# Neighbourhood attention with 192 keys in its edge blocks, a shared transpose for the remainders, later pieces of the weight sums, and two adds of the feed-forward products moved to VectorE

## The chip, the cores and the metric

The kernel runs on one core of one Trainium2 chip. The metric is the device time of one execution in microseconds (us). Before the change it was 1300.42 us, the median of three runs (1299.76 to 1302.81).

## The reference, cut to what matters

The reference is a two-layer encoder over 512 tokens of width 1024, all in f32. The tokens form a grid of 8 rows by 64 columns. Each layer does three residual steps. The first is a mixer, which adds the output of eight heads of neighbourhood attention and of eight heads of grouped-query attention. The second is a cross-attention over 256 memory tokens, and the third a feed-forward block with a gated unit, a convolution of width three over the positions and two products. The step that the change rewrites is the neighbourhood attention: each query sees all 8 rows and a window of 16 columns, clamped at the borders.

```
row_start = clip(r - kh // 2, 0, rows - kh)            # kh = 8 = rows: all rows
col_start = clip(c - NA_KW // 2, 0, GRID_W - NA_KW)    # NA_KW = 16
col_valid = (c[None] >= col_start[:, None]) & (c[None] < col_start[:, None] + NA_KW)
scores = q.k * dh ** -0.5 + bias[h, row_off, col_off]
scores = where(col_valid, scores, -1e30)
o = softmax(scores, over rows and columns) . v
```

## The kernel before, in words

**Tiling.** The tokens are reordered column by column, so 128 tokens are 16 columns of all 8 rows. The 512 queries make four blocks of 128. The keys that a block's queries can see lie in at most 32 columns, so each block takes a window of 256 keys that starts at key 0, 64, 192 or 256 (`WIN`, line 48). Blocks 0 and 3 lie at the border: the last 64 keys of block 0's window and the first 64 of block 3's are beyond the reach of every query, and their bias is -1e30.

**Number format.** All large products are made of f32 operands that are split into a high and a low part (hi is a rounded copy, made by ScalarE, lo is the difference, made by VectorE or GpSimd); three products hi·hi, hi·lo, lo·hi are summed in PSUM (`mm3`, line 939). Weights come from HBM into a `raw` tile and are split by `emit_split` (lines 801 and 802).

**Units of the neighbourhood attention.** A unit is a pair of heads and a pair of query blocks, so 8 units per layer and 16 in all; `bp` = 0 has blocks 0 and 1, `bp` = 1 has blocks 2 and 3, so each unit has one edge block and one inner block. A unit has four steps. `na_scores` (line 1405) makes eight score matmuls, then for each head and block one VectorE operation that adds the bias and takes the maximum over 256 columns (line 1423), and one exponential on ScalarE (line 1429). `na_normalise` (line 1433) scales the four blocks by the reciprocal sums, one on ScalarE and three on GpSimd (line 1106). `na_transpose` (line 1444) makes four 128x128 transposes per head on TensorE into one PSUM bank (line 1451), which ScalarE and VectorE split into hi and lo (lines 1099 and 1100). `na_values` (line 1459) makes eight value matmuls and folds the results (lines 1475 to 1477).

**The value tiles.** For each group of four heads (`g` = 0 and 1) the values, split into hi and lo, lie in four tiles `vs[0..3]` of two blocks of 128 keys each. `vs[0]` and `vs[1]` hold the keys from 0, 128, 256 and 384. `straddle` (line 1390) copies halves of them between partitions, with five DMAs, to the blocks that start at keys 64, 192 and 320 (`vs[2]` and the first half of `vs[3]`). The second half of `vs[3]` is unused.

**What sets the order.** `weave` (line 196) calls the unit's steps in a software pipeline; between them a filler runs other matmuls (projections, memory values, output rows), paced by `NA_FILL`. Work that must come later is put in `late`, a list with due times in TensorE nanoseconds (n times `LATE` = 3600). All DMAs of SP keep the written order. For the compute engines a planner (class `Order`, line 359) simulates the whole program with its own cost figures, with random draws from a fixed seed, and fixes the order of TensorE, VectorE, ScalarE and GpSimd from the best of its rounds; any change of the program makes it plan all of it anew.

**Weight sums.** The feed-forward products from tile 4 on use sums and differences of weight quarters. `make_form` (line 717) makes one piece of them in HBM: SP issues a copy (line 730), and GpSimd issues an accumulating DMA on it (line 731). Pieces are made at given steps of the stages: in both layers' neighbourhood attention at steps 0 to 4 of ten (line 1733), then in the later stages. In the first layer, steps 0 to 6 also run `mem_stat` (line 1157), which loads the memory tokens with SP in four pieces and squares each on ScalarE (line 1164).

**Feed-forward products.** `up_forms` (line 1977) combines partial products per tile `j` (4 to 21, 18 per layer). At two places a half bank is copied from PSUM to SBUF by ScalarE (lines 2033 and 2045), GpSimd adds another half to it (lines 2034 and 2046), and VectorE adds the result into a bank (lines 2035 and 2047).

Of the kernel before, what the change touches and what calls it, by code (L numbers as in the profile page):

```python
# [11 lines left out]
F32 = mybir.dt.float32  # L12
F32R = mybir.dt.float32r
AF = mybir.ActivationFunctionType
# [33 lines left out]
WIN = [0, 64, 192, 256]  # L48
WTYPE = [0, 1, 1, 2]

# [6 lines left out]

NA_FILL = [[2800] * 6 + [1500] * 4, [2800] * 6 + [1400] * 4]
GQA_SLOT = [3750] * 16 + [4200, 3300]
MEM_FILL = [1, 1, 2, 2, 1, 3, 1, 3, 1, 3, 1]  # L60
# [635 lines left out]
def encoder_kernel(ctx: ExitStack, tc: tile.TileContext, t: dict, out: bass.AP):  # L696
# [521 lines left out]
    for l in range(DEPTH):  # L1218
# [6 lines left out]
        def load_bias(p):  # L1225
            bias[p] = [rtile((4, 256), F32) for _ in range(2)]
            for j in range(2):
                SP.dma_start(bias[p][j][:, 0:3, :], t["bias"][l, 2 * p + j])

# [160 lines left out]
        def straddle(g, vs):  # L1390
            straddled[g] = True
            for dst, src in (
                (vs[2][0:64, 0:2], vs[0][64:128, 0:2]),
                (vs[2][64:128, 0], vs[0][0:64, 1]),
                (vs[2][64:128, 1], vs[1][0:64, 0]),
                (vs[3][0:64, 0], vs[1][64:128, 0]),
                (vs[3][64:128, 0], vs[1][0:64, 1]),
            ):
                SP.dma_start(f(dst), f(src))


# [3 lines left out]
        def na_scores(u):  # L1405
# [11 lines left out]
            nmx, sums = small(4), small(4)  # L1417
            es = [tmp((2, 256)) for _ in range(2)]
            for j in range(2):
                for i in range(2):  # L1420
                    b = 2 * bp + i
                    col = slice(2 * j + i, 2 * j + i + 1)
                    DVE.tensor_tensor_reduce(  # L1423
                        out=sc[j][:, i, :], in0=sc[j][:, i, :], in1=bias[p][j][:, WTYPE[b], :],
                        op0=ALU.add, op1=ALU.min, scale=-1.0, scalar=BIG, accum_out=nmx[:, col])
            for j in range(2):
                for i in range(2):
                    col = slice(2 * j + i, 2 * j + i + 1)
                    ACT.activation(es[j][:, i, :], sc[j][:, i, :], AF.Exp, bias=nmx[:, col], scale=-1.0,  # L1429
                                   accum_out=sums[:, col])  # L1430
            na[u] = es, sums

        def na_normalise(u):
            es, sums = na[u]
            DVE.reciprocal(sums, sums)
            for j in range(2):
                for i in range(2):
                    if i or j:
                        normalise(es[j][:, i, :], sums, 2 * j + i, POOL)
                    else:  # L1440
                        ACT.activation(es[j][:, i, :], es[j][:, i, :], AF.Copy, scale=sums[:, 2 * j + i : 2 * j + i + 1])
            na[u] = es

        def na_transpose(u):
            es = na[u]
            pts = []
            for j in range(2):
                tr = ps_t()
                for i in range(2):
                    for c in range(2):  # L1450
                        PE.transpose(tr[:, (2 * i + c) * P : (2 * i + c + 1) * P], es[j][:, i, c * P : (c + 1) * P], ident)  # L1451
                pt = rtile((2, S))
                split_psum(pt[:, 0, :], pt[:, 1, :], tr)
                pts.append(pt)
            na[u] = pts

        o32s = {}

        def na_values(u):
# [7 lines left out]
            for j in range(2):  # L1467
                po = ps_mm().rearrange("p (i n q) -> p i n q", i=2, n=2)
                for i in range(2):
                    b = 2 * bp + i  # L1470
                    for c in range(2):
                        PE.matmul(po[:, i], vblk[p // 2][WIN[b] + P * c][:, 2 * (p % 2) + j, :],
                                  pts[j][:, :, (2 * i + c) * P : (2 * i + c + 1) * P], start=c == 0, stop=c == 1)
# [252 lines left out]
        def na_quanta(s):  # L1726
# [250 lines left out]
        def up_forms(j):  # L1977
# [66 lines left out]
            product(c, "diffs", 0, "b22", False)  # L2044
            ACT.copy(vc, cl)  # L2045
            POOL.tensor_add(vc, vc, u2)  # L2046
            DVE.tensor_add(bl, ch, vc)
# [178 lines left out]
def _bias_index():  # L2226
# [11 lines left out]
    return np.broadcast_to(ro[:, None, :], ci.shape), ci  # L2238

# [42 lines left out]
```

## Time and profile before

| what | value |
|---|---|
| median of three runs | 1300.42 us (1299.76 to 1302.81) |
| the profiled execution's own time | 1298.67 us |
| its span, first to last instruction | 1296.9 us |
| TensorE (PE) busy | 1285.7 us, 6731 matmuls |
| VectorE (DVE) busy | 919.5 us |
| ScalarE (ACT) busy | 786.9 us |
| GpSimd (POOL) busy | 861.0 us |
| mean granted TensorE clock | 0.999 |
| DMA moved | 241.22 MB, mean 186 GB/s |

The profile names engines PE (matmul), PEld (weight load), DVE (VectorE), ACT (ScalarE), POOL (GpSimd) and SP (SyncE, which issues DMAs); a name with a q at its end is the engine's sequencer. An instruction is told as line, engine, operation, out<-in. L103 is the helper line behind which all counted matmuls stand; L80 is that for operations that keep the written order, the DMAs of SP among them. Ends of matmuls are modelled and overlap, so the distance from one start to the next tells what a matmul costs, and the duration does not.

### The profile page before, as it was taken

The numbers are of one execution on the slowest core, as the hardware profiler recorded it, in microseconds if no ns is written. First come the engines' busy times: TensorE is split into PE (matmuls) and PEld (weight loads), VectorE is DVE, ScalarE is ACT, GpSimd is POOL, SyncE is SP. The second block draws the span as 40 slices with busy tenths as digits, with TensorE's granted clock in tenths as the row PEclk, the third lists the DMA queues.
The fourth block names the chain that finished last, engine by engine and source line by source line (L and its number), as shares of the span: only waits on it lengthen the run. The fifth ranks groups of instructions, "written<-read, shape, count | busy, mean of one in ns | idle before, by whom it ended". The sixth has DMA issues, their size and how long they took to land.

```text
span 1296.9 us, 19575 instructions
## 1 busy us (share of the span) xinstructions
PE 1285.7 (99%) x6731; PEld 1093.9 (84%) x6731; DVE 919.5 (71%) x1727; ACT 786.9 (61%) x1487; POOL 861.0 (66%) x656
## 2 busy tenths in 40 slices
PE   9999999999999999999999999999999999999997
PEld 8888888888888888888888888888888888888887
DVE  6568977677986765866635697776789767667565
ACT  6667867566655654554636687765656556456444
POOL 3658966736777776766746579757367766667663
PEclk9999999999999999999999999999999999999999
DMA  9998496497985465554459965946988855555441
GB/s 290 283 281 202 131 246 144 151 257 195 244 210 146 140 179 146 166 159 131 146 164 270 287 152 159 240 109 225 219 223 207 206 155 158 162 158 154 144 134 65
DMA packets 293698, 241.22 MB, mean 186 GB/s; under 512 B 7776, under 2 KB 249952, under 8 KB 293600
## 3 DMA queue, kind: packets, MB, share of 16 engines
q1 hardware_dynamic: 276288, 201.83, 51.7%
q0 software_dynamic: 16896, 37.75, 16.2%
q8 instruction: 53, 0.87, 0.3%
q10 hardware_dynamic: 416, 0.39, 0.1%
q14 instruction: 45, 0.37, 0.1%
HBM read 229.99 MB, written 77.59 MB: 237 GB/s over the span
## 4 chain that ended last, share of the span: by engine, by line
PE 95%; DVE 2%; ACT 1%; DMA 1%; issue 0%; POOL 0%; POOLq 0%; SPq 0%; DVEq 0%; ACTq 0%
PE mm L103 69%; PE sc L103 18%; PE tr L103 5%; PE tr L1606 2%; PE tr L1451 1%; PE tr L1802 1%; DMA r<-r 0%; DVE sc L1423 0%; PE tr L1521 0%; DVE r L1317 0%; DMA xT<-in_xT 0%; DVE r L1300 0%; ACT t L1429 0%; ACT hi L801 0%; DVE r L1100 0%
## 5 line engine op out<-in xcount | busy, mean ns | idle before, releaser
L802 POOL TENSOR_TENSOR lo<-raw,hi 128x512 fp32r<-128x512 f32 (+3 forms) x329 | 576.4, 1769 | 257.1 <-ACT hi L801 209.9
L801 ACT CAST hi<-raw 128x1024 fp32r<-128x1024 f32 (+2 forms) x369 | 295.5, 815 | 273.3 <-issue 64.8
L103 PE MATMUL mm<-r,hi 128*128 128x512 f32 (+1 forms) x1376 | 419.3, 389 | 0.0
L103 PEld LDWEIGHTS mm<-r,hi 128*128 128x128 f32 x1376 | 249.4, 188 | 43.9
L103 PE MATMUL mm<-r,lo 128*128 128x512 f32 (+1 forms) x864 | 261.9, 345 | 0.0
L103 PE MATMUL mm<-xg,hi 128*128 128x512 f32 x768 | 228.0, 392 | 0.0
L103 PEld LDWEIGHTS mm<-r,lo 128*128 128x128 f32 x864 | 152.1, 188 | 26.6 <-DVE lo L802 1.7
L103 PEld LDWEIGHTS mm<-xg,hi 128*128 128x128 f32 x768 | 140.6, 188 | 26.7
L103 PE MATMUL mm<-xg,lo 128*128 128x256 f32 (+1 forms) x528 | 139.5, 331 | 0.0
L103 PE MATMUL mm<-hi,xg 128*128 128x512 f32 (+1 forms) x384 | 111.1, 360 | 1.5 <-DVE r L1300 1.5
L103 PEld LDWEIGHTS mm<-xg,lo 128*128 128x128 f32 x528 | 89.2, 188 | 15.4
L1106 POOL TENSOR_SCALAR t<-t,s 128x512 f32<-128x512 f32 (+1 forms) x112 | 67.5, 620 | 41.4 <-DVE s L1590 21.1
L2046 POOL TENSOR_TENSOR t<-t 128x256 f32<-128x256 f32 x36 | 43.1, 1197 | 71.9 <-ACT t L2045 71.9
L103 PE MATMUL sc<-xg,hi 128*128 128x512 f32 x304 | 88.8, 393 | 0.2 <-ACT xg L80 0.2
L103 PEld LDWEIGHTS mm<-hi,xg 128*128 128x128 f32 x384 | 68.1, 189 | 10.6 <-DVE r L1300 1.7
L802 DVE TENSOR_TENSOR lo<-raw,hi 128x1024 fp32r<-128x1024 f32 (+1 forms) x40 | 54.5, 1362 | 31.2 <-ACT hi L801 31.2
L103 PE MATMUL sc<-r,r 128*128 128x256 f32 (+1 forms) x352 | 74.1, 331 | 0.0
L1099 ACT CAST r<-tr 128x512 fp32r<-128x512 f32 x79 | 45.5, 587 | 37.9 <-DVE tr L1916 27.0
L103 PE MATMUL mm<-lo,xg 128*128 128x512 f32 (+1 forms) x192 | 68.5, 357 | 0.0
L2053 DVE TENSOR_TENSOR sc<-mm,t 128x256 f32<-128x256 f32 x36 | 15.6, 432 | 74.1 <-ACT t L2052 74.1
L103 PEld LDWEIGHTS sc<-xg,hi 128*128 128x128 f32 x304 | 55.0, 189 | 10.7 <-ACT xg L80 0.5
L1100 DVE TENSOR_TENSOR r<-tr,r 128x512 fp32r<-128x512 f32 x79 | 53.4, 685 | 13.0 <-ACT r L1099 9.4
(232 smaller groups left out, 2389.9 us busy)
## 6 DMA issues: line engine op xcount, KB each, us to landing
raw<-in_w_up SPq DMA_DIRECT2D x52, 512.0 KB, 4.6
raw<-dr_sums SPq DMA_DIRECT2D x36, 512.0 KB, 4.0
raw<-dr_diffs SPq DMA_DIRECT2D x36, 512.0 KB, 4.1
raw<-in_w_in SPq DMA_DIRECT2D x25, 512.0 KB, 6.2
raw<-in_w_down SPq DMA_DIRECT2D x32, 384.0 KB, 3.8
dr_sums<-in_w_up SPq DMA_DIRECT2D x8, 1280.0 KB, 8.6
dr_diffs<-in_w_up SPq DMA_DIRECT2D x8, 1280.0 KB, 8.6
raw<-in_w_up SPq DMA_DIRECT2D x36, 256.0 KB, 3.2
```

The source lines that it names most:

```text
L103: return self.engine.matmul(out, lhsT, rhs, **k)
L801: act.copy(hi[:, k], raw[:, k])
L802: (POOL if eng[0] == "P" else DVE).tensor_sub(lo[:, k], raw[:, k], f(hi)[:, k])
L1099: ACT.copy(hi, ps)
L1100: DVE.tensor_sub(lo, ps, f(hi))
L1106: eng.tensor_scalar(e, e, sums[:, col : col + 1], 1.0, op0=ALU.mult, op1=ALU.mult)
L1451: PE.transpose(tr[:, (2 * i + c) * P : (2 * i + c + 1) * P], es[j][:, i, c * P : (c + 1) * P], ident)
L1606: PE.transpose(tr[:, k * P : (k + 1) * P], es[j][:, k * P : (k + 1) * P], ident)
L1802: PE.transpose(tr[:, (2 * c + i) * P : (2 * c + i + 1) * P], e[:, i, c * P : (c + 1) * P], ident)
L2046: POOL.tensor_add(vc, vc, u2)
L2053: DVE.tensor_add(ch, ah, l4)
```

## The change

Block 0 uses keys 0 to 191 and block 3 keys 320 to 511, which is 192 keys. The score matmuls stay 256 wide, but the bias addition, the exponential and the normalisation of an edge block take 192 columns, and the bias array in HBM has 640 columns for its three kinds of block where it had 768. The two heads' edge blocks lie side by side in one tile (`edge`, 384 columns). 192 keys are one transpose of 128 and a remainder of 64; the remainders of the two heads are neighbours in `edge` and go through one transpose, so a unit has 7 transposes where it had 8, and the second bank to be split is 384 wide. The value matmul of the remainder has 64 keys of the one head and 64 of the other on its partitions. So its stationary operand (`rest`) has the head's own values on 64 partitions and zeros on the other 64. `heads_apart` makes such a block with six DMAs: two copies of values and four of zeros. The block for the lower edge goes into the unused half of `vs[3]`, directly after `straddle`. The block for the upper edge goes over the keys from 128 in `vs[0]`, which no value matmul reads any more, three `late` steps after that, or when unit 1 of the group of four has been transposed. The number of value matmuls is still eight.

The pieces of the weight sums in the first layer's neighbourhood attention move from steps 0 to 4 to steps 3 to 7; the second layer keeps steps 0 to 4. In `up_forms`, for tiles from 7 on (15 of 18 per layer), the copy by ScalarE and the addition by GpSimd become one addition by VectorE, at both places.

```diff
+KEYS = [slice(0, 192), slice(0, 256), slice(0, 256), slice(64, 256)]
+EDGE = {0: (0, 64), 3: (320, 384)}
+BIAS = [slice(0, 192), slice(192, 448), slice(192, 448), slice(448, 640)]
...
+REST = 3
+NA_SUMS = [(3, 4, 5, 6, 7), (0, 1, 2, 3, 4)]
...
+    zeros = cpool.tile([P, 64], F32R, name="zeros")
+    DVE.tensor_sub(zeros, ident[:, 0:64], ident[:, 0:64])
...
+            kept_vs[g] = vs
+            rest[g][0] = vs[3][:, 1]
+            heads_apart(vs[3][:, 1], (vs[0][0:64, 1], vs[0][0:64, 0]))
+            late(REST, lambda: last_rest(g, vs))
...
+        def heads_apart(dst, srcs):
+            dst = dst.rearrange("p (a j) d -> p a j d", j=2)
+            for j, src in enumerate(srcs):
+                src = src.rearrange("p (a j) d -> p a j d", j=2)
+                r, o = slice(64 * j, 64 * j + 64), slice(64 - 64 * j, 128 - 64 * j)
+                SP.dma_start(f(dst[r, :, j]), f(src[:, :, j]))
+                for i in range(2):
+                    SP.dma_start(f(dst[o, :, j, 64 * i : 64 * i + 64]), f(zeros[o].unsqueeze(1).to_broadcast([64, 2, 64])))
+
+        def last_rest(g, vs):
+            if rest[g][1] is None:
+                rest[g][1] = vs[0][:, 1]
+                heads_apart(vs[0][:, 1], (vs[1][64:128, 1], vs[1][64:128, 0]))
...
-                        out=sc[j][:, i, :], in0=sc[j][:, i, :], in1=bias[p][j][:, WTYPE[b], :],
+                        out=sc[j][:, i, ks], in0=sc[j][:, i, ks], in1=bias[p][j][:, BIAS[b]],
...
-                for i in range(2):
-                    for c in range(2):
-                        PE.transpose(tr[:, (2 * i + c) * P : (2 * i + c + 1) * P], es[j][:, i, c * P : (c + 1) * P], ident)
+                ins = [es[j][1 - bp][:, 0:P], es[j][1 - bp][:, P : 2 * P], edge[:, 256 * j : 256 * j + P], edge[:, P : 2 * P]]
+                n = len(ins) - j
+                for c, e in enumerate(ins[:n]):
+                    PE.transpose(tr[:, c * P : c * P + P], e, ident)
...
+                    if b in (0, 3):
+                        assert rest[p // 2][bp] is not None
+                        vs = [(vblk[p // 2][EDGE[b][j]], pts[j], 2), (rest[p // 2][bp], pts[0], 3)]
+                    else:
+                        vs = [(vblk[p // 2][WIN[b] + P * c], pts[j], c) for c in range(2)]
...
-            if s in (0,1,2,3,4,):
+            if s in NA_SUMS[l]:
                 make_form()
...
-            ACT.copy(gb, bl)
-            POOL.tensor_add(gb, gb, p1)
+            if j < 7:
+                ACT.copy(gb, bl)
+                POOL.tensor_add(gb, gb, p1)
+            else:
+                DVE.tensor_add(gb, bl, p1)
...
-            ACT.copy(vc, cl)
-            POOL.tensor_add(vc, vc, u2)
+            if j < 7:
+                ACT.copy(vc, cl)
+                POOL.tensor_add(vc, vc, u2)
+            else:
+                DVE.tensor_add(vc, cl, u2)
```

More of the change, by code (lines that the diff above doesn't have):

```diff
@@ L1225, in load_bias @@
         def load_bias(p):
-            bias[p] = [rtile((4, 256), F32) for _ in range(2)]
+            bias[p] = [rtile((1024,), F32) for _ in range(2)]
             for j in range(2):
-                SP.dma_start(bias[p][j][:, 0:3, :], t["bias"][l, 2 * p + j])
+                SP.dma_start(bias[p][j][:, 0:640], t["bias"][l, 2 * p + j])
         def project_first():
@@ L1417, in na_scores @@
             nmx, sums = small(4), small(4)
-            es = [tmp((2, 256)) for _ in range(2)]
+            inner, edge = tmp((2, 256)), tmp()
+            es = [[edge[:, 192 * j : 192 * j + 192] if i == bp else inner[:, j] for i in range(2)] for j in range(2)]
+            for j in range(2):
+                for i in range(2):
+                    b = 2 * bp + i
+                    col, ks = slice(2 * j + i, 2 * j + i + 1), KEYS[b]
+                    DVE.tensor_tensor_reduce(
+                        out=sc[j][:, i, ks], in0=sc[j][:, i, ks], in1=bias[p][j][:, BIAS[b]],
+                        op0=ALU.add, op1=ALU.min, scale=-1.0, scalar=BIG, accum_out=nmx[:, col])
             for j in range(2):
@@ L1422, in na_scores @@
                     col = slice(2 * j + i, 2 * j + i + 1)
-                    DVE.tensor_tensor_reduce(
-                        out=sc[j][:, i, :], in0=sc[j][:, i, :], in1=bias[p][j][:, WTYPE[b], :],
-                        op0=ALU.add, op1=ALU.min, scale=-1.0, scalar=BIG, accum_out=nmx[:, col])
-            for j in range(2):
-                for i in range(2):
-                    col = slice(2 * j + i, 2 * j + i + 1)
-                    ACT.activation(es[j][:, i, :], sc[j][:, i, :], AF.Exp, bias=nmx[:, col], scale=-1.0,
+                    ACT.activation(es[j][i], sc[j][:, i, KEYS[b]], AF.Exp, bias=nmx[:, col], scale=-1.0,
                                    accum_out=sums[:, col])
-            na[u] = es, sums
+            na[u] = es, edge, sums
         def na_normalise(u):
-            es, sums = na[u]
+            es, edge, sums = na[u]
             DVE.reciprocal(sums, sums)
@@ L1438, in na_normalise @@
                     if i or j:
-                        normalise(es[j][:, i, :], sums, 2 * j + i, POOL)
+                        normalise(es[j][i], sums, 2 * j + i, POOL)
                     else:
-                        ACT.activation(es[j][:, i, :], es[j][:, i, :], AF.Copy, scale=sums[:, 2 * j + i : 2 * j + i + 1])
-            na[u] = es
+                        ACT.activation(es[j][i], es[j][i], AF.Copy, scale=sums[:, 2 * j + i : 2 * j + i + 1])
+            na[u] = es, edge
         def na_transpose(u):
-            es = na[u]
-            pts = []
+            es, edge = na[u]
+            pts, bp = [], u % 2
             for j in range(2):
                 tr = ps_t()
-                for i in range(2):
-                    for c in range(2):
-                        PE.transpose(tr[:, (2 * i + c) * P : (2 * i + c + 1) * P], es[j][:, i, c * P : (c + 1) * P], ident)
+                ins = [es[j][1 - bp][:, 0:P], es[j][1 - bp][:, P : 2 * P], edge[:, 256 * j : 256 * j + P], edge[:, P : 2 * P]]
+                n = len(ins) - j
+                for c, e in enumerate(ins[:n]):
+                    PE.transpose(tr[:, c * P : c * P + P], e, ident)
                 pt = rtile((2, S))
-                split_psum(pt[:, 0, :], pt[:, 1, :], tr)
+                split_psum(pt[:, 0, : n * P], pt[:, 1, : n * P], tr[:, : n * P])
                 pts.append(pt)
             na[u] = pts
+            if u % 4 == 1:
+                last_rest(u // 4, kept_vs[u // 4])
         o32s = {}
@@ L1470, in na_values @@
                     b = 2 * bp + i
-                    for c in range(2):
-                        PE.matmul(po[:, i], vblk[p // 2][WIN[b] + P * c][:, 2 * (p % 2) + j, :],
-                                  pts[j][:, :, (2 * i + c) * P : (2 * i + c + 1) * P], start=c == 0, stop=c == 1)
+                    if b in (0, 3):
[3 more added lines that the diff above has]
+                        vs = [(vblk[p // 2][WIN[b] + P * c], pts[j], c) for c in range(2)]
+                    for c, (v, pt, n) in enumerate(vs):
+                        PE.matmul(po[:, i], v[:, 2 * (p % 2) + j, :], pt[:, :, n * P : n * P + P], start=c == 0, stop=c == 1)
                 r = slice(64 * j, 64 * j + 64)
@@ L2237, in _bias_index @@
         ci[:, y] = np.where((k0 + kc >= s0) & (k0 + kc < s0 + 16), dc + 15, 31)
-    return np.broadcast_to(ro[:, None, :], ci.shape), ci
+    ro = np.broadcast_to(ro[:, None, :], ci.shape)
+    return tuple(np.concatenate([v[:, 0, :192], v[:, 1], v[:, 2, 64:]], axis=1) for v in (ro, ci))
 def kernel(**inputs):
```

2 lines of the change are left out of this document (1 added, 1 removed).

## The prediction

> **What bounds the kernel.** I read the page first: how full the engines are, and the chain that ended last.
>
> ```profile
> span 1296.9 us, 19575 instructions
> ...
> PE 1285.7 (99%) x6731; PEld 1093.9 (84%) x6731; DVE 919.5 (71%) x1727; ACT 786.9 (61%) x1487; POOL 861.0 (66%) x656
> ...
> PE 95%; DVE 2%; ACT 1%; DMA 1%; issue 0%; POOL 0%; POOLq 0%; SPq 0%; DVEq 0%; ACTq 0%
> ```
>
> TensorE is busy for 99% of the span and holds 95% of the chain. So only two things shorten the time: fewer TensorE instructions, or less of TensorE's idle time, which is 1296.9 - 1285.7 = 11.2 us. Work taken from VectorE, ScalarE or GpSimd counts only where TensorE waits for it. Second I asked who TensorE waited for (us in total, times, longest):
>
> ```profile
> PE mm L103 <- DVE r L1300: 1.5, 1, 1.5
> PE tr L103 <- POOL ident masks.py:199: 1.4, 1, 1.4
> PE tr L1451 <- DVE r L1317: 0.8, 1, 0.8
> PE tr L1606 <- DVE r L1317: 0.4, 1, 0.4
> PE mm L103 <- POOL lo L802: 0.3, 1, 0.3
> ```
>
> The 1.4 us is the start, before the change has any say. The other four make 3.0 us. Third, busy time by stretches (us; PE, PEld, DVE, ACT, POOL, the clock, DMA share, GB/s), to see where the idle time lies:
>
> ```profile
> 50.00:75.00 25.00, 23.55 (x123) 19.93 (x122) 15.01 (x37) 15.85 (x39) 19.81 (x22) 1.00 1.07 317
> 100.00:125.00 25.00, 24.00 (x142) 20.37 (x141) 22.01 (x56) 18.46 (x52) 19.02 (x22) 1.00 0.91 215
> 125.00:150.00 25.00, 25.00 (x131) 20.68 (x131) 23.91 (x48) 21.87 (x45) 23.86 (x23) 1.00 0.49 145
> 450.00:625.00 175.00, 175.00 (x907) 149.04 (x906) 115.90 (x186) 90.79 (x141) 121.17 (x73) 1.00 0.54 152
> 750.00:775.00 25.00, 24.71 (x147) 20.79 (x146) 23.98 (x57) 20.56 (x50) 17.83 (x21) 1.00 0.61 121
> 775.00:800.00 25.00, 24.63 (x125) 20.01 (x124) 22.54 (x46) 22.34 (x47) 23.59 (x23) 1.00 0.46 144
> 1275.00:1296.90 21.90, 15.32 (x106) 13.90 (x104) 9.90 (x24) 10.70 (x27) 5.64 (x6) 0.95 0.27 96
> ```
>
> The last row holds 21.9 - 15.32 = 6.6 us of the idle time, at the end of the program, which the change leaves as it is. The first layer's neighbourhood attention loses 1.45 + 1.0 us, the same stage of the second layer 0.29 + 0.37 us. In the feed-forward stretch from 450 to 625 TensorE is idle for nothing. So at most some 3 us of waits can be had, all in the two attention stages.
>
> **Part 1: the transposes.** Instructions in order of time, and the row of the line:
>
> ```profile
> 94.05 1.07 PE L1451 MATMUL tr<-ident,t 128*128 128x128 f32 x8
> 94.87 0.49 PE L103 MATMUL mm<-hi,xg 128*128 128x512 f32 x1
> ...
> L1451 PE MATMUL tr<-ident,t x128: 270/272/328, 58.9 to 771.3; 128*128 128x128 f32 x128
> ```
>
> The 128 are 16 units of 8. One lasts 272 ns, but eight of them and the step to the next product take 94.87 - 94.05 = 0.82 us, so one costs 0.10 us of TensorE's time; from inside the run of eight it is (1.07 - 0.27) / 7 = 0.114 us. I take 0.108. Sixteen fewer save 16 x 0.108 = **1.7 us** (1.6 to 1.8). Score and value matmuls keep their number and width, so nothing else leaves TensorE. The Trainium skill (TensorE: Matmul & The Clock Gate, Part 4: PE-mode transpose) tells about 275 ns for a 128x128 transpose inside a kernel. Taken as the price, that would be 4.4 us; the row has the same duration, but the next start comes after 0.10 us, so it is no price here.
>
> **Part 2: narrower edge blocks.** Rows of VectorE and ScalarE (count, busy us, mean ns of one):
>
> ```profile
> L1423 DVE CUSTOM_DVE_ANT_0 sc<-sc,r 128x256 f32<-128x256 f32 x64 | 25.5, 452 | 8.9 <-PE sc L103 8.6
> L1100 DVE TENSOR_TENSOR r<-tr,r 128x512 fp32r<-128x512 f32 x79 | 53.4, 685 | 13.0 <-ACT r L1099 9.4 <-PE mm L103 3.3
> L1100 DVE TENSOR_TENSOR r<-mm,r 128x256 fp32r<-128x256 f32 x8 | 3.3, 416 | 0.9 <-ACT r L1099 0.9
> ```
>
> From 256 to 512 columns VectorE takes 685 - 416 = 269 ns more, 1.05 ns a column. Half of the 64 bias operations lose 64 columns (67 ns each) and one of two splits per unit loses 128 (134 ns): 0.27 us per unit, 4.3 us in all, with savings of the same kind on ScalarE and GpSimd. VectorE is at 22.0 and 23.9 of 25 us from 100 to 150 us, and there TensorE waits 0.8 us for its L1317 and 0.4 us again. Some three units fall there in each layer; 3 x 0.27 = 0.8 us of room. Bounds 0 to -1.2 us; I take **-0.6**, half.
>
> **Part 3: the pieces moved in the first layer.** The 1.5 us wait ended at 72.42 us. What the stage did before:
>
> ```profile
> 51.13 0.53 SPq L80 DMA_DIRECT2D dr_sums<-in_w_up  x1
> ...
> 52.89 0.46 SPq L80 DMA_DIRECT2D t<-in_memT  x1
> 53.51 0.52 SPq L80 DMA_DIRECT2D dr_diffs<-in_w_up  x1
> ...
> 61.43 0.64 ACT L1164 ACTIVATE t<-t 128x512 f32<-128x512 f32 x1 [1.37 <-DMA t<-in_memT]
> 63.18 0.69 DVE L1100 TENSOR_TENSOR r<-tr,r 128x512 fp32r<-128x512 f32 x1 [3.19 <-ACT r L1099]
> 70.95 1.41 DVE L1300 TENSOR_TENSOR r<-mm,r 64x512 fp32r<-64x512 f32 x2 [1.45 <-ACT r L1296]
> 72.42 0.50 PE L103 MATMUL mm<-hi,xg 128*128 128x512 f32 x1 [1.45 <-DVE r L1300]
> ```
>
> ScalarE stood 1.37 us in its order before L1164, for a memory load issued at 52.89 that landed at 61.4, 8.5 us later, with the DMA engines full (1.07, 317 GB/s). The rows before and behind it are copies for two pieces. VectorE then waited for ScalarE, ScalarE's next evictions were late, and TensorE lost 1.45 us. At steps 3 to 7 the first pieces come behind this load. If it lands 1.4 us earlier, the wait goes whole. Against it, the new DMAs of part 4 stand ahead of this load on SP. Bounds 0 to -1.5; I take **-1.2**.
>
> What is moved is five SP issues (0.52 us each above) and five on GpSimd:
>
> ```profile
> L731 POOL DMA_DIRECT2D dr_sums<-in_w_up x8 | 8.9, 1108 | 0.0
> ```
>
> About three of them now fall from 100 to 150 us: 3 x 1.1 = 3.3 us of GpSimd's time, where it has 50 - 19.0 - 23.9 = 7.1 us idle. I cost them at nothing; without that cover, the lo parts of weights (L802) are late by up to 3.3 us.
>
> **Part 4: the remainder blocks.** `heads_apart` is called four times per layer, with six DMAs: 24 more on SP per layer. Their nearest rows:
>
> ```profile
> 101.26 3.43 SPq L80 DMA_DIRECT2D r<-r  x5
> 104.78 0.55 SPq L80 DMA_DIRECT2D raw<-in_w_out  x1
> ...
> r<-r SPq DMA_DIRECT2D x8, 128.0 KB, 7.4
> ...
> 112.47 1.12 PE L103 MATMUL mm<-r,r 128*128 128x256 f32 x8
> ```
>
> Five such copies took 3.43 us to issue, so six take 4.1 us. Behind them on SP stand the raw weights, the copies of k and the memory loads. Raw weights are loaded as soon as one of five buffers is free and wait for GpSimd's lo, so 4 us there is hidden. The critical one is the first layer's second group: the copies of `straddle` were issued until 104.69 and take 7.4 us to land, about 112, and the first value products of that group start at 112.47. The lower-edge block is issued behind them, so it lands some 4.1 us later, at 116. Only the edge half of that unit needs it, and the planner can put filler products there. Bounds 0 to +4.1 us per layer, +8.2 for two; I take **+0.3**, near the lower end, because the planner knows these DMAs and TensorE's stretch here is more than half filler. The Trainium skill (DMA: Bandwidth & Descriptors, Rules for kernel authors) says to join small transfers, since under 64 KB one pays mostly overhead; by that these 24 are a bad trade. The trace agrees that size hardly matters here: 128 KB took 7.4 us.
>
> **Part 5: the feed-forward adds.** Fifteen of 18 tiles per layer, two places each, lose a copy and an add and gain one add, like L2043:
>
> ```profile
> L2043 DVE TENSOR_TENSOR t<-mm,t 128x256 f32<-128x256 f32 x36 | 15.1, 419 | 0.4
> L2045 ACT COPY t<-sc 128x256 f32<-128x256 f32 x36 | 13.2, 368 | 0.5
> L2046 POOL TENSOR_TENSOR t<-t 128x256 f32<-128x256 f32 x36 | 43.1, 1197 | 71.9 <-ACT t L2045 71.9
> ```
>
> VectorE gains 60 x 0.419 = 25 us, some 10 us of it in the 175 us from 450 to 625, where it has 59 us free. TensorE waits for nothing there, so the price is nothing in either direction; if VectorE were full, up to 10 us per layer would be at stake. The zero tile (one subtraction of 64 columns) costs the start 0.2 us at most; I take nothing.
>
> **The sum.** -1.7 - 0.6 - 1.2 + 0.3 = -3.2 us. The profiled execution took 1298.67 us (1.8 outside its span) and would take 1295.5. It is 1.75 us under the median of the three runs, so the forecast against the median is 1300.42 - 3.2 = **1297.2 us**, 0.25% less. About 0.3% is what a measurement of this kernel tells from no change, 3.9 us: faster means below 1296.5, slower above 1304.3.
>
> **Rivals.** *All waits go.* The planner orders anew with lighter engines and the 3.0 us vanish beside the 1.7: 1295.7; with the shorter holes that the wait list leaves out, 1294.5. For it: the second layer loses only 0.66 us with the same code, so 2.4 of the 3.0 are luck of order and of DMA load. Against it: VectorE stays above 21 of 25 us from 100 to 150.
>
> *The waits move.* The 24 DMAs fill the gap that the pieces leave, the memory load is as late as before, VectorE's stretch keeps its waits, a new order adds 1 to 2 us (the difference of the two layers shows this size): only the 1.7 is left, or nothing: 1298.7 to 1300.4.
>
> *The remainder is late.* TensorE stands at the edge product of the second group's first unit until the block lands, 4.1 us in each layer, and the moved pieces, now in flight at the same time, lengthen the 7.4 us landing by 2 us more: 8.2 + 2 - 1.7 = +8.5, 1308.9. For it: the landing at 112 and the product at 112.47 stand 0.5 us apart. It decides once the block lands later than the filler reaches, that is if fewer than 4 us of other products are ready at that place. Against it: the projections for the grouped attention run in these very microseconds.
>
> **How the numbers follow.** The forecast has 0.5, with its own range 1295.3 to 1299; about a third of that, 0.17, lies under 1296.5. All waits go 0.23, the waits move 0.16, the remainder is late 0.11. Faster is 0.23 + 0.17 = 0.40, same 0.33 + 0.16 = 0.49, slower 0.11. The range reaches from 1293.5 to 1302.0: below, all waits with the shorter holes; above, moved waits and a part of the late remainder.
>
> **What would show it.** L1451 x112 and 1.7 us less of it; edge forms of 192 columns at the bias line and the exponential; no wait of ScalarE for the memory load before 72 us, and 50 to 75 at 25 of 25; the values of the second group no later than their neighbours; the feed-forward adds of GpSimd x6 per place, and TensorE without a gap there. I am wrong if a wait for a DMA appears before a value product, if GpSimd's lo becomes TensorE's wait after 100 us, or if the saving is more than the transposes and the listed waits together.

## The result, and the profile after

The changed kernel takes 1316.45 us (median of four runs, 1314.93 to 1319.16), the kernel before 1300.1 us on the same chip. The ratio is 1.0131, with a 95% interval from 1.0116 to 1.0146: it became **slower by 1.3%**, 16 us, where the forecast was 1297.2 and the upper end of the range 1302.0. The profiled execution took 1314.93 us. Its span is 16.3 us longer than that of before. The page of the changed kernel:

```profile
span 1313.2 us, 19545 instructions
...
PE 1286.8 (98%) x6715; PEld 1096.0 (83%) x6715; DVE 942.1 (72%) x1788; ACT 767.6 (58%) x1427; POOL 803.5 (61%) x596
...
PEclk9998999999999999999999989999999999999999
...
PE 88%; DMA 6%; DVE 1%; POOL 1%; issue 1%; ACT 1%; SPq 1%; POOLq 0%; ACTq 0%; DVEq 0%
```

TensorE's idle time is now 1313.2 - 1286.8 = 26.4 us, where it was 11.2: 15.2 us more. Its busy time rose by 1.1 us although it has 16 instructions less. The granted clock shows two dips (fourth and 24th slice), and DMA holds 6% of the chain where it held 1%. Who TensorE waited for (us in total, times, longest):

```profile
PE mm L107 <- DMA r<-zeros: 16.5, 3, 10.5
PE tr L107 <- POOL ident masks.py:199: 1.4, 1, 1.4
PE mm L107 <- DVE t L1512: 0.9, 2, 0.5
PE tr L1641 <- DVE r L1323: 0.5, 1, 0.5
PE tr L1480 <- DVE r L1323: 0.3, 1, 0.3
```

Without the 1.4 us of the start this makes 18.2 us, where before had 3.4 (the 3.0 of the prediction's rows and two waits of 0.2 that it does not show): 14.8 more, nearly the whole growth of the idle time. 16.5 of the 18.2 are waits of a new kind, for the zeros that `heads_apart` writes by DMA into a remainder block. Five of the prediction's stretches (PE, PEld, DVE, ACT, POOL, the clock, DMA share, GB/s):

```profile
50.00:75.00 25.00, 25.00 (x134) 21.43 (x133) 15.78 (x42) 15.71 (x39) 18.60 (x21) 1.00 0.92 281
100.00:125.00 25.00, 17.64 (x105) 15.03 (x103) 20.57 (x49) 14.03 (x39) 16.70 (x20) 0.92 0.98 263
125.00:150.00 25.00, 21.11 (x107) 17.71 (x108) 16.83 (x32) 16.00 (x35) 15.44 (x16) 0.87 0.47 132
450.00:625.00 175.00, 175.00 (x918) 149.91 (x917) 125.74 (x211) 85.82 (x118) 99.08 (x52) 1.00 0.54 153
750.00:775.00 25.00, 19.55 (x114) 16.63 (x113) 21.09 (x55) 13.87 (x37) 18.97 (x23) 0.96 0.99 226
```

The early wait of the first layer is gone (25.00 of 25 from 50 to 75), the feed-forward stretch is as full as before, and the loss sits where the second group's edge products stand, at the same place in both layers. The instructions of TensorE there, in order of time, and those behind the wait:

```profile
117.07 0.60 PE L1556 MATMUL tr<-ident,t 128*128 128x128 f32 x4
117.43 0.60 PE L107 MATMUL mm<-r,r 128*128 128x256 f32 x3
128.54 0.55 PE L107 MATMUL mm<-r,r 128*128 128x256 f32 x1 [10.52 <-DMA r<-zeros]
...
130.60 1.02 PE L107 MATMUL mm<-hi,xg 128*128 128x512 f32 x2
131.46 0.41 PE L107 MATMUL mm<-lo,xg 128*128 128x512 f32 x1
...
132.60 0.39 PE L107 MATMUL mm<-lo,xg 128*128 128x512 f32 x1
132.83 0.63 PE L107 MATMUL mm<-hi,xg 128*128 128x512 f32 x2
```

Three value products, then 10.5 us of nothing until the third of the block's six DMAs has landed, at 128.41 (the first head's half needs these three). After it, two products of 512 columns take 131.46 - 130.60 = 0.86 us, 0.43 each; from 132.60 they take 0.23 again. That is half the clock for some 3 us: the granted clock from 128.54 to 131.47 us is 0.50. In the second layer TensorE waits 1.7 us (until 770.47) and 4.3 us (until 775.52), and from 775.52 to 780.00 its clock is 0.50 again. Half of these 2.9 and 4.5 us, 3.7 us, is what the slow clock costs by this estimate. From the busy time one gets 2.8: with -1.7 for the transposes it makes the +1.1 seen. So it is some 3 to 4 us. The Trainium skill (TensorE: Matmul & The Clock Gate, Why this matters for your kernels) says that an idle gap of over about 3 us brings the half clock back; both long waits here are followed by it, so the trace agrees.

The DMAs issued from 111.55 to 115.56 us, the last remainder block of the second group among them (out<-in, queue, count, KB each, median us from issue to landing):

```profile
dr_sums<-dr_sums POOLq DMA_DIRECT2D x1, 1024.0 KB, 12.5
dr_diffs<-in_w_up SPq DMA_DIRECT2D x1, 1024.0 KB, 12.4
r<-r SPq DMA_DIRECT2D x2, 64.0 KB, 14.6
r<-zeros SPq DMA_DIRECT2D x4, 32.0 KB, 15.0
```

32 KB took 15 us to land. Two large transfers were under way beside it, an accumulating DMA of GpSimd (issued at 110.45) and a plain copy of SP (at 111.02), both for pieces of the weight sums. In the second layer two accumulating DMAs were issued at 759.60 and 760.36, SP had no piece's copy in front, and the six copies issued from 760.59 on landed one after the other at 767.26, 768.87, 770.33, 772.04, 773.68 and 775.43.

Sums in this stretch are not new. The kernel before issued two of them at nearly the same time, and TensorE waited there for no DMA:

```profile
112.71 1.14 POOL L731 DMA_DIRECT2D dr_diffs<-dr_sums  x1
113.46 1.44 POOL L731 DMA_DIRECT2D dr_sums<-in_w_up  x1
```

New are the block that has to land beside them and, in the first layer, SP's copy of a piece just ahead of it.

### The profile page after: what moved, and what is told of

It is laid out like the page before. It is cut to its first block, busy times and chain, and to the rows that moved or that the text cites. A ratio compares the mean times of both kernels' runs of the same rounds, so it can differ in the third digit from the quotient of the medians.

```text
span 1313.2 us, 19545 instructions
## 1 busy us (share of the span) xinstructions
PE 1286.8 (98%) x6715; PEld 1096.0 (83%) x6715; DVE 942.1 (72%) x1788; ACT 767.6 (58%) x1427; POOL 803.5 (61%) x596
## 4 chain that ended last, share of the span: by engine, by line
PE 88%; DMA 6%; DVE 1%; POOL 1%; issue 1%; ACT 1%; SPq 1%; POOLq 0%; ACTq 0%; DVEq 0%
PE mm L107 63%; PE sc L107 17%; PE tr L107 5%; DMA r<-zeros 3%; PE tr L1641 2%; DMA dr_sums<-in_w_up 2%; SPq L84 1%; POOL lo L806 1%; DMA r<-r 1%; DMA raw<-in_w_in 1%; PE tr L1837 1%; PE tr L1480 0%; ACT hi L805 0%; DVE r L1323 0%; DVE r L1106 0%
## 5 line engine op out<-in xcount | busy, mean ns | idle before, releaser
L1112 POOL TENSOR_SCALAR t<-t,s 128x512 f32<-128x512 f32 (+2 forms) x112 | 66.2, 607 | 62.1 <-DVE s L1463 30.9
L1105 ACT CAST r<-tr 128x512 fp32r<-128x512 f32 (+1 forms) x79 | 43.7, 564 | 39.4 <-DVE tr L1951 28.6
L107 PEld LDWEIGHTS sc<-xg,hi 128*128 128x128 f32 x304 | 55.1, 189 | 10.5 <-ACT xg L84 0.5
L1106 DVE TENSOR_TENSOR r<-tr,r 128x512 fp32r<-128x512 f32 (+1 forms) x79 | 51.3, 659 | 16.5 <-ACT r L1105 16.0
L107 PE MATMUL sc<-r,hi 128*128 128x512 f32 x208 | 61.9, 397 | 0.0
L1619 ACT ACTIVATE t<-sc,s,qr 128x512 f32<-128x512 f32 x64 | 49.4, 779 | 21.0 <-DVE s L1112 20.6
L2039 DVE TENSOR_REDUCE t<-mm 128x256 f32<-128x512 f32 x72 | 49.4, 686 | 15.1 <-PE mm L107 14.9
```

The source lines that it names most:

```text
L107: return self.engine.matmul(out, lhsT, rhs, **k)
L1105: ACT.copy(hi, ps)
L1106: DVE.tensor_sub(lo, ps, f(hi))
L1112: eng.tensor_scalar(e, e, sums[:, col : col + 1], 1.0, op0=ALU.mult, op1=ALU.mult)
L1619: ACT.activation(e, sc[j], AF.Exp, bias=nmx[:, c], scale=qrs[b][:, col : col + 1], accum_out=sums[:, c])
L2039: DVE.tensor_reduce(dst, bank.rearrange("p (n c) -> p c n", n=2), axis=AX.X, op=ALU.add)
```

## The experiments

The question was why this block lands late. The theories were, in the order in which they came up: the **count** (six DMAs per block instead of two, through SP's eight semaphores in rotation), the **queue** (the 1 MB copy for a piece stands ahead of the block on SP's queue), and the **sums** (GpSimd's accumulating DMA, in flight at the same time). Each ratio is to the kernel before in the same session, which took 1298.9 us beside half_rows, no_edge, pieces_back and zeros_by_pool; 1300.64 beside half_rows_paired, idle_dmas, rest_from_act and pieces_away; 1299.16 beside sums_held, extra_copy and zeros_by_pool_held; and 1298.91 beside one_sum_ahead.

**half_rows: no zeros at all.** The remainder is multiplied by a 64-row matmul on its own half of the partitions, and two copies of `straddle` per group replace the twelve DMAs.

```diff
...
+                        vs = [(vblk[p // 2][EDGE[b][j]], pts[j], 2, slice(0, P)),
+                              (own, pts[0], 3, slice(64 * j, 64 * j + 64))]
...
-                        PE.matmul(po[:, i], v[:, 2 * (p % 2) + j, :], pt[:, :, n * P : n * P + P], start=c == 0, stop=c == 1)
+                        PE.matmul(po[:, i], v[h, 2 * (p % 2) + j, :], pt[h, :, n * P : n * P + P], start=c == 0, stop=c == 1)
```

> The whole change, but the shared remainder is multiplied by values that stand on 64 partitions alone, so no zeros and no block of its own are needed: two more copies in the straddle step take the place of twelve DMAs per group, and all are issued before the pieces that come later. Queue theory (TensorE stands for remainder DMAs that lie in SP's queue behind a 1 to 1.3 MB copy of a piece): no wait for the remainder, 1294 to 1299 us. Number theory (twelve small DMAs per group are too many for SP): the same, 1294 to 1299. Order theory (a new order of the engines costs the time, the DMA is only the last to come): stays above 1305.

1304.28 us, ratio 1.0041 [1.0030, 1.0052]. No wait of TensorE for a remainder is left. What stayed is a new price. TensorE's eight value products of a unit, and the group of the 64-row ones:

```profile
66.21 1.89 PE L106 MATMUL mm<-r,r 128*128 128x256 f32 x8
67.93 0.39 PE L106 MATMUL mm<-hi,xg 128*128 128x512 f32 x1
...
L106 PE MATMUL mm<-r,r 64*128 64x256 f32 x32 | 12.2, 381 | 0.0
```

The eight take 67.93 - 66.21 = 1.72 us, where they took 0.95 before; two of them are 64-row products, so one adds (1.72 - 0.95) / 2 = 0.385 us, and 32 of them 12.3 us. TensorE's busy time shows it: 1294.0 us. So the loss of the changed kernel does hang on these DMAs, and most of what this version saves on them it pays to TensorE.

**half_rows_paired.** The two 64-row products of a unit stand next to each other, behind the six others.

```diff
+                        if b in (0, 3) and c == 1:
+                            last.append(one)
+                        else:
+                            PE.matmul(*one[:3], start=c == 0, stop=c == 1)
+            for one in last:
+                PE.matmul(*one[:3], start=False, stop=True)
```

> half_rows with the unit's two 64-row products moved next to each other, behind the six full ones, so that a unit has one run of half-array products where it had two. In half_rows each 64-row product was followed by a start 0.19 us late and preceded by another (eight value products took 1.72 us where they took 0.95). If the price is for the change between full and half array: it halves, 16 times 0.38 us, 6 us less, 1297 to 1300. If it is a price of each 64-row product: no change, 1303 to 1305.

1300.32 us, ratio 0.9998 [0.9988, 1.0009]; TensorE busy 1289.8 us. Half as many changes between full and half rows cost some 4 us less, of the 6 expected. The eight products of a unit, issued from 66.35 us, take 1.12 us until the next one starts, where they took 1.72. So most of the price belongs to the change from the one form to the other, and little to the product.

**no_edge: the moved pieces and the feed-forward adds alone.** The kernel before with parts 3 and 5.

```diff
-            if s in (0,1,2,3,4,):
+            if s in ((3, 4, 5, 6, 7), (0, 1, 2, 3, 4))[l]:
                 make_form()
...
+                DVE.tensor_add(gb, bl, p1)
...
+                DVE.tensor_add(vc, cl, u2)
```

> The kernel before with only the other two parts: the first layer's pieces at steps 3 to 7 and the adds on VectorE for tiles from 7 on. No edge blocks of 192 keys. Queue and number theory: no remainder, so no such wait; 1296 to 1300 us, the first layer's stretch from 50 to 75 us without idle time of TensorE. Order theory: slower than 1303.

1297.82 us, ratio 1.0002 [0.9987, 1.0018]. Six of ten runs lay at 1297.1 to 1297.9, four at 1302.2 to 1302.6; the profiled one was of the latter and waited 3.8 us for VectorE's r L1317. From 50 to 75 us TensorE is busy for 25.00 of 25. So the two parts don't bring the loss, but no gain is seen either: in the profiled execution, what the moved pieces gain in the first stretch comes back as other waits.

**pieces_back: the whole change, with the pieces of the first layer at steps 0 to 4.**

```diff
-NA_SUMS = [(3, 4, 5, 6, 7), (0, 1, 2, 3, 4)]
+NA_SUMS = [(0, 1, 2, 3, 4), (0, 1, 2, 3, 4)]
```

> The whole change, but the first layer's pieces at steps 0 to 4 as before. Queue theory: no SP copy of a piece is issued just ahead of the last remainder block in the first layer, so its 10.5 us wait falls to at most the 6.3 us that the second layer has with the same steps: 1309 to 1313 us. Number theory: the twelve DMAs are still there, the wait stays 9 to 11 us: 1315 to 1317.

1320.37 us, ratio 1.0166 [1.0136, 1.0195]: not better, as the queue theory had it, but worse. The DMAs issued from 121.0 to 125.2 us, with the last remainder block:

```profile
dr_sums<-in_w_up POOLq DMA_DIRECT2D x1, 1024.0 KB, 13.9
raw<-in_w_out SPq DMA_DIRECT2D x1, 512.0 KB, 12.6
r<-r SPq DMA_DIRECT2D x1, 256.0 KB, 12.7
r<-r SPq DMA_DIRECT2D x2, 64.0 KB, 13.8
r<-zeros SPq DMA_DIRECT2D x4, 32.0 KB, 13.9
```

No copy of SP for a piece is among them, and the block takes 14 us all the same. What is there is an accumulating DMA of GpSimd (issued at 122.19, another at 119.33): SP's copies had moved, but GpSimd's sums stood at this place again, as in the kernel before. Beside that, TensorE lost 3.9 + 1.4 us before 91 us, and ScalarE stood 3.33 and 3.35 us for the memory load: what part 3 said of the pieces at steps 0 to 4 is seen here.

**zeros_by_pool: GpSimd writes the zeros, two DMAs per block.**

```diff
-                for i in range(2):
-                    SP.dma_start(f(dst[o, :, j, 64 * i : 64 * i + 64]), f(zeros[o].unsqueeze(1).to_broadcast([64, 2, 64])))
+                for a in range(2):
+                    POOL.tensor_copy(dst[o, a, j, :].rearrange("p (i d) -> p i d", i=2), zeros[o].unsqueeze(1).to_broadcast([64, 2, 64]))
```

> The whole change, but the zeros are written by GpSimd (four copies of 64 partitions by 128 columns per block) and only the two copies of values per block are DMAs. Number theory: a third of the DMAs is left and the waits of 16.5 us fall to a third: 1303 to 1307 us. Queue theory: the two copies lie behind the same piece and land only the time of four zero fills earlier, 2 to 3 us per layer: 1309 to 1314.

1296.67 us, ratio 0.9979 [0.9968, 0.9990], less than either theory gave. The two copies of the last block were issued at 111.67 and 112.32 and landed after 5.7 us; the accumulating DMA came only at 115.73. SP's copy of a piece still stood ahead of them (109.33). Two things had changed at once, the count and the moment of GpSimd's sums.

**idle_dmas: the count alone.** zeros_by_pool with four DMAs of 16 bytes per partition per block, into a tile that nothing reads.

```diff
...
+                    SP.dma_start(f(spare[o, c]), f(zeros[o, 0:4]))
...
```

> zeros_by_pool (zeros written by GpSimd, 1296.67 us) with four DMAs per block put back that move nothing of use: 16 bytes on each of 64 partitions into a spare tile that nothing reads. Slot theory (SP has eight DMAs in flight; each further issue waits until the one eight places before has landed, so the four extra DMAs per block push the copies of values, and what stands behind them, later by several us): the waits for the remainder come back, to 1308 to 1317 us. Data theory (what costs is that the value products need the zeros' own landing): nothing waits for these DMAs, so the time stays 1296 to 1299.

1297.94 us, ratio 0.9984 [0.9970, 0.9998]; the interval overlaps that of zeros_by_pool. Six DMAs per block on SP again, and 1.6 us of waits in all, for the copies of values. The count by itself is not the cause. The rule that the prediction weighed, to join small transfers (the Trainium skill, DMA: Bandwidth & Descriptors, Rules for kernel authors), would have had 32 more of them in the kernel cost something; beside the measurement's own spread they cost 1.3 us or nothing.

**rest_from_act: the last block's six DMAs on ScalarE's queue.**

```diff
-        def heads_apart(dst, srcs):
+        def heads_apart(dst, srcs, by=SP):
...
-                heads_apart(vs[0][:, 1], (vs[1][64:128, 1], vs[1][64:128, 0]))
+                heads_apart(vs[0][:, 1], (vs[1][64:128, 1], vs[1][64:128, 0]), ACT_IN_ORDER)
```

> The whole change, but the six DMAs of the last block of each group are issued by ScalarE's queue; the first block's six stay on SP. Slot theory: the block stands neither behind SP's eight slots nor behind a piece on SP's queue and lands in some 3 to 8 us from its issue; the waits of TensorE for it fall under 3 us and the time to 1297 to 1303 (ScalarE pays 24 issues of about 0.6 us). If instead the DMA engines are simply full at that time, whoever issues: the landing stays over 12 us, 1310 or more.

1320.99 us, ratio 1.0164 [1.0143, 1.0184]. The waits of TensorE:

```profile
PE mm L107 <- DVE r L1106: 15.1, 2, 14.5
PE mm L107 <- DMA r<-zeros: 5.8, 2, 3.5
```

The block's copies, issued from 114.29 to 132.6 us:

```profile
r<-r ACTq DMA_DIRECT2D x2, 64.0 KB, 7.0
r<-zeros ACTq DMA_DIRECT2D x4, 32.0 KB, 6.4
```

So the other queue does help the landing, as the slot theory had it: 6 to 7 us at the median, with two of GpSimd's sums in flight (issued at 109.88 and 117.09), where SP's queue took 15. What came late were the issues: 114.29, 114.98, 115.62, then 121.21, 127.57 and 132.03. In the trace ScalarE's DMAs use the same eight semaphores as SP's, and the last three issues each came 0.02 us after a DMA of SP had landed: raw weights at 121.19, copies for two pieces at 127.55 and 132.01. ScalarE stood in its own order at these issues, so its evictions were late, VectorE's split behind them, and TensorE 14.5 us behind that. An engine with a part in the chain should not issue DMAs that may have to wait.

**pieces_away: no pieces in the neighbourhood attention.** All pieces of the two stages move to the steps of the grouped attention.

```diff
-NA_SUMS = [(3, 4, 5, 6, 7), (0, 1, 2, 3, 4)]
+NA_SUMS = [(), ()]
...
-            if s in (0,4,8,12,):
+            if s in (0, 2, 4, 6, 8, 10, 12, 14, 15):
```

> The whole change, with no piece of the weight sums made in the neighbourhood attention of either layer; the five go to the grouped attention with its four. The 24 small DMAs per layer stay. Queue theory in its strong form (the pieces' big copies are what the remainder waits for): the waits vanish, 1295 to 1300. Slot theory: the big copies no longer hold slots for 8 to 12 us, so most of the wait goes too, but issues still wait for weight loads eight places before: a wait of 1 to 5 us is left, 1298 to 1304. Number of issues alone (12 times 0.65 us of SP's time): the waits stay over 10 us, 1310 or more.

1305.08 us (1302.54 to 1311.7), ratio 1.0047 [1.0028, 1.0065]. No wait for a remainder is left. The DMAs issued from 111.6 to 116.4 us:

```profile
r<-r SPq DMA_DIRECT2D x2, 64.0 KB, 3.2
r<-zeros SPq DMA_DIRECT2D x4, 32.0 KB, 2.2
```

The same six copies on the same queue land in 2 to 3 us with neither SP's copies nor GpSimd's sums about. The time was lost elsewhere: the pieces crowd the later stage, where loads took over 20 us. What this kernel can't tell is which of the two, copy or sum, made the difference.

**sums_held: the whole change, GpSimd's accumulating DMAs taken out of the stage.** SP's copies stay where they were; the sums are kept and issued one per step of the grouped attention.

```diff
-        nc.gpsimd.dma_start(dst, more, accum_op=ALU.add, max_dma_last_dim=4 * P * nj)
+        held.append((dst, more, nj))
+        if not holding[0]:
+            accumulate(len(held))
...
+    def accumulate(n):
+        for dst, more, nj in held[:n]:
+            POOL_IN_ORDER.dma_start(dst, more, accum_op=ALU.add, max_dma_last_dim=4 * P * nj)
+        del held[:n]
...
+            accumulate(1)
             return [GQA_SLOT[s]]
```

> The whole change, with its 24 small DMAs per layer and its steps for the pieces, but GpSimd's accumulating DMAs of the pieces are held back in written order and issued one per step of the grouped attention; SP's copies of the pieces stay where they are. Accumulate theory (a remainder block issued while a GpSimd accumulate of 1 MB is in flight lands 6 to 17 us after its issue, one issued before it lands in 2 to 6): no accumulate is in flight, the waits for the remainder fall from 16.5 to under 5 us, 1297 to 1304. Queue theory (SP's own copy of a piece ahead of it is what it waits for): that copy is still 0.5 us ahead in the first layer, so 8 us or more of wait stay there, 1308 to 1314.

1296.13 us, ratio 0.9970 [0.9958, 0.9982]: 20 us less than the changed kernel, with all its 48 DMAs and the copy ahead of the block. Its DMAs issued from 111.4 to 115.4 us, and its wait for the block:

```profile
dr_diffs<-in_w_up SPq DMA_DIRECT2D x1, 1024.0 KB, 7.9
r<-r SPq DMA_DIRECT2D x2, 64.0 KB, 6.7
r<-zeros SPq DMA_DIRECT2D x4, 32.0 KB, 6.0
```

```profile
PE mm L107 <- DMA r<-zeros: 1.9, 1, 1.9
```

Against the rows of the changed kernel: the same copy of SP ahead, 6.0 us instead of 15.0, 1.9 us of wait instead of 16.5; the time lies below the range of either theory. So the queue alone does not make the block late, and the sums, or the new order of work that came with holding them, do. The queue still has a part in the first layer. The block lands right behind SP's copy of the piece, here at 118.93 to 119.73 behind 118.77, in the changed kernel at 125.15 to 129.65 behind 123.43. With the sums in flight that copy took 12.4 us instead of 7.9, and the block behind it was late with it.

**extra_copy: the queue alone.** zeros_by_pool with a plain copy of 1 MB, which nothing reads, issued by SP just ahead of the last block.

```diff
...
             if rest[g][1] is None:
+                SP.dma_start(spare_copy[l][g], t["w_up"][l][:512, 0:512])
```

> zeros_by_pool (1296.67 us) with one more copy of 1 MB from HBM to HBM on SP directly ahead of the copies of the last block, in both groups of both layers; nothing reads it. Queue theory: the block lands behind it, some 5 to 8 us later; the second group's waits come back with 3 to 7 us per layer, 1302 to 1311. Accumulate theory: a copy alone takes about 6 us and the block lands behind it too, but only where its product is that near: 1298 to 1304.

1295.21 us, ratio 0.9966 [0.9952, 0.9980], below the range of either theory. The DMAs from 108.9 to 111.8 us:

```profile
dr_diffs<-in_w_up SPq DMA_DIRECT2D x1, 1024.0 KB, 7.5
dr_spare<-in_w_up SPq DMA_DIRECT2D x1, 1024.0 KB, 10.1
r<-r SPq DMA_DIRECT2D x2, 64.0 KB, 8.5
```

Two megabytes ahead on the same queue instead of one make the block land after 8.5 us instead of 5.7, and TensorE wait 1.2 us. That is the price of the queue without a sum: the next one was issued at 114.82, 3.6 us behind the block's last copy.

**zeros_by_pool_held: both remedies.** zeros_by_pool with the held sums of sums_held (the two diffs together).

> A version meant to be the best: zeros by GpSimd (1296.67 us) and the accumulates held to the grouped attention. Both theories: no wait for the remainder, and the DMA engines emptier until 145 us: 1294 to 1297. If the held accumulates get in the way of the weights of the grouped attention instead: 1298 or more.

1297.88 us, ratio 0.9990 [0.9982, 0.9999]. They don't add up: with no late block left to cure, what remains is the order that the planner finds, here with 1.6 us of wait for VectorE's t L1522 and 1.5 for r L1333.

**one_sum_ahead: one accumulating DMA put back.** sums_held, and in each layer one sum of 1 MB into a buffer that nothing reads, issued by GpSimd just ahead of the second group's last block. (One plain copy fills the buffer first, in the first layer's first group.)

```diff
             if rest[g][1] is None:
...
+                if g == 1:
+                    POOL_IN_ORDER.dma_start(spare_sum, src, accum_op=ALU.add, max_dma_last_dim=4 * P * 4)
```

> The kernel with the held sums (1296.13 us, last remainder block of the second group landed 8 us after its issue), and in it one single accumulating DMA of GpSimd, 1 MB of f32, into a buffer that nothing reads, issued just ahead of the last remainder block of the second group in each layer: two such DMAs in all. The output is the same. Theory (an accumulating DMA in flight stretches the landing of the small copies beside it): the block lands 12 to 17 us after its issue, TensorE waits for it for 6 to 17 us over the two layers and runs slower for a few us after each wait; 1303 to 1315. Rival (it was the planner's order or the traffic as a whole that the holding of the sums changed): the block lands within 8 us as before, at most 3 us of wait; 1295 to 1299.

1308.78 us, ratio 1.0075 [1.0058, 1.0092]: 12.7 us more than sums_held for two DMAs. The DMAs from 113.05 to 119.1 us, with the block, and the wait:

```profile
dr_diffs<-in_w_up SPq DMA_DIRECT2D x1, 1024.0 KB, 11.4
r<-r SPq DMA_DIRECT2D x2, 64.0 KB, 9.3
r<-zeros SPq DMA_DIRECT2D x4, 32.0 KB, 7.8
```

```profile
PE mm L107 <- DMA r<-zeros: 8.8, 4, 5.6
```

From the first issue to the last landing the block takes 12 us in the first layer (113.1 to 125.1), and two of its issues take 1.76 and 1.24 us instead of 0.6. The landings themselves lengthen by less than the 12 to 17 us expected, and by less than in the changed kernel, which has a second sum close behind the first in each layer. TensorE's idle time is 7.0 us above that of sums_held and its busy time 5.7 us (granted clock 0.89 from 125 to 150 us): the half clock is nearly half of the price. Holding the sums back had also changed the order of work. That rival expected at most 3 us of wait and 1295 to 1299 us here, and falls.

The second layer shows the sums by themselves, because there SP has no copy of a piece ahead of the block. The zeros of the second group's last block in the second layer, with no sum (sums_held), one (one_sum_ahead) and two (the changed kernel):

```profile
r<-zeros SPq DMA_DIRECT2D x4, 32.0 KB, 2.5
```

```profile
r<-zeros SPq DMA_DIRECT2D x4, 32.0 KB, 8.2
```

```profile
r<-zeros SPq DMA_DIRECT2D x4, 32.0 KB, 9.4
```

## Why the prediction was wrong, step by step

**The step that failed** is part 4, the remainder blocks at +0.3 us with bounds 0 to +8.2. It measured +16.5 us of waits and some 3 to 4 us of half clock behind them, for which the sum had no term. The bound was made of the wrong things: the time that six issues take on SP (4.1 us; the six did take 3.9) and the landing time of 128 KB copies as the page of before shows them, 7.4 us. The second is not a property of the copy (the same page has 256 KB in 3.2 us and 512 KB in 4.6). It depends on what is in flight beside it: 2 to 3 us in pieces_away, 6 in sums_held, 15 in the changed kernel.

Part 3 counted about three of GpSimd's five DMAs as coming into 100 to 150 us, and asked only for GpSimd's time (3.3 us, with 7.1 free). But two were there before (112.71 and 113.46) and two after (110.45 and 117.66). What they do to the transfers beside them was never asked, though the trace of before had them within a microsecond of the first value product at 112.47. The rival of the late remainder did name the mechanism, TensorE standing at an edge product with the pieces in flight, and gave them 2 us where the landing grew by 9 (from 6.0 to 15.0); it got 0.11.

Part 4 also followed the wrong block. It worked out 116 for the lower-edge block of the second group's first unit, which landed at 111.6, and no wait for it is in the list. The second one, which `last_rest` writes behind it on SP, was the late one, at the unit after. The prediction gave that one no landing time and no first use of its own.

**The cover failed too.** "The planner knows these DMAs" was a reason for the lower end. The order it found has sums issued within 1.2 us of the block in both layers, and beside it again in pieces_back. And the filler of "more than half" of that stretch was used up: three products of the unit ran, then TensorE stood.

**Right by mechanism and size.** Part 1: the transposes are x112, and in versions without the late block TensorE is busy for 1282.1 us (extra_copy), 1283.1 (sums_held) and 1284.3 (zeros_by_pool) where it was 1285.7 before; 1.7 us less lies inside this spread, which settles it no closer. The row's duration of 272 ns (4.4 us for 16) does not. Part 2: the bias operation of 192 columns takes 373 ns against 442, and the split of 384 columns 546 against 688, as worked out; what that is worth to TensorE no run shows alone. Part 3: TensorE's wait before 72 us is gone in the changed kernel and back, at 3.9 us, in pieces_back; ScalarE's own wait for the memory load only fell, from 1.37 to 0.88 us, and no_edge shows no gain in time. Part 5: VectorE rose from 115.9 to 125.7 us of the 175 (123.4 from 460 to 635, since the work itself came later by about 10 us), near the 10 us forecast, and TensorE has no gap there.

**The sum without the late block** came out near the measurements, in part by luck. 1297.2 less the 0.3 is 1296.9, a ratio of 0.9973 to 1300.42. The versions that cure the block and bring no other price have 0.9966 (extra_copy), 0.9970 (sums_held), 0.9979 (zeros_by_pool), 0.9984 (idle_dmas) and 0.9990 (zeros_by_pool_held). But parts 3 and 5 by themselves gave 1.0002 [0.9987, 1.0018] in no_edge, where -1.2 us would be 0.9991: that neither confirms nor refutes the term, and the total confirms no single one. The changed kernel thus contains a gain of 0.1 to 0.3% and a loss of some 1.5%. Both sums_held and extra_copy beat both kernels; extra_copy does so with a copy that serves nothing, so 1 to 2 us among these versions is order or spread, not merit. One figure of the range does not follow: the rival with the shorter holes gives 1294.5, and the lower end was put at 1293.5.

**What stays open.** How close ahead a sum must be issued to make a block late: in idle_dmas one was issued (115.15) between the six DMAs of the block, and they landed after 4.3 to 6.8 us; in zeros_by_pool it came 3.4 us behind the block. Two copies per block with a sum just ahead of them were not tried. And why the planner puts the sums there is not known from these runs.

## What to carry to other kernels

A landing time read from a profile holds for the traffic that was in flight with it; before a small transfer is made critical, look for what the change, or the scheduler, can put beside it, and above all for accumulating DMAs. Follow every block that a new helper writes to its own first use, the last one in the queue first, not only the one that looks tightest. And price a stall of TensorE of 3 us or more with the slow clock behind it (the shortest lone wait followed by it here is 3.0 us, in no_edge): that was some 3 to 4 of 20 us in the changed kernel and 5.7 of 12.7 in one_sum_ahead.

## What was not expected of the hardware

Copies of 32 KB on SP's queue, behind one or two of GpSimd's accumulating DMAs of 1 MB, landed in 8 to 9 us instead of 2.5 where no copy of a piece stood ahead on their own queue (second layer), and in 8 to 15 us instead of 6 behind a plain copy of 1 MB (first layer). One more plain copy of 1 MB ahead on the same queue cost some 3 us. This is no rule for all copies: on ScalarE's queue they landed in 6 to 7 us (medians of the first layer) with two sums in flight (rest_from_act), and the copies of `straddle` in the changed kernel took 8 to 9 us (issued from 99.14, landed by 109.83) with no sum in flight. In the second layer of the changed kernel the six copies land 1.5 to 1.8 us apart, where five copies of `straddle` just before landed 0.3 to 0.5 us apart (757.94 to 759.55). The Trainium skill (DMA: Bandwidth & Descriptors, Queues, rings and completion order) says that each DMA engine takes turns between the queues by whole packets; copies that land one by one at equal steps beside GpSimd's sums agree with that, but no run here isolates the packets.

A matmul with 64 rows between matmuls with 128 costs TensorE 0.385 us more than one with 128 (32 of them 12.3 us), most of it for the change of form: set side by side in pairs, eight products took 1.12 us instead of 1.72, and TensorE was 4.2 us less busy (1294.0 to 1289.8).
